# In the gated MLP of an encoder block, GpSimd makes the third convolution tap, most sums of values and two of three weight sums

## The chip, the cores and the metric

One core of one Trainium2 chip runs the whole kernel. The metric is the device time of an execution in microseconds (us), the median over runs. The engines are TensorE (PE; its weight loads are PEld), VectorE (DVE), ScalarE (ACT), GpSimd (POOL) and SyncE (SP), which issues nearly all DMAs.

## What is computed

An encoder block on 272 tokens (256 and 16 meta tokens) of width 2048, all in float32: a normalised input projection, neighbourhood attention on 8 heads and latent attention on 8 heads, an output projection, and a gated MLP of width 5632 with a convolution over positions on the gate. The change lies in the MLP:

```python
def conv_glu(x, w_gate, w_up, conv_w, conv_b, w_down):
    g = x @ w_gate
    u = x @ w_up
    gp = jnp.pad(g, ((0, 0), (pad, pad), (0, 0)))
    gc = conv_b
    for i in range(CONV_W):                 # CONV_W = 3 taps
        gc = gc + conv_w[i] * gp[:, i:i + L]
    return (jax.nn.silu(gc) * u) @ w_down
```

## The kernel before

**Numbers in two parts.** Every float32 product is made of matmuls on a high part (`hi`, `whi`: ScalarE rounds to the matmul's type) and a low part (`lo`, `wlo`: VectorE subtracts the high part from the value). A product takes three matmuls (`mm3`, L734 to L736; `product3` through `MM`, L291) or two (`mm2`, L2056 and L2057). So each weight that is loaded (tiles `raw`) is read once by ScalarE (`split_hi`, the helper at L251) and once by VectorE (`split_lo`, the helper at L255) before TensorE may use it. There are 4 buffers each for `whi` and `wlo` and 5 for `raw`; a buffer is given back when TensorE has used the piece.

**Products with sums.** Twenty of the 44 tiles of the up projection are made in five groups of four ("quads", `QUADS`), and most of the down projection in a similar way, by a scheme that multiplies 2 x 2 blocks with seven products instead of eight. For that it needs sums of weights and sums of the other operand. `weight_sums` (L633 on) makes, for each of 8 row pairs of a quad, one sum on 512 columns and two on 256 columns in a tile of the slots `made` (before the change one tile, `more_raw`); this tile is then split like a loaded weight. `value_sums` makes the sums of the MLP's values for the down projection: four operations on 128 columns and, after ScalarE's high parts, two subtractions on 256 columns into the tile `sums`, which a DMA saves (`pair_sums` calls it for each pair of value tiles; the sums of the last pairs, from `LAST - 3` on, are needed soon after). The sums of the normalised input are made once, by `hl_sums`; some are kept in room of the tile `act` that is not yet in use (`near`), others are saved and loaded again when a row pair needs them. `near_to(g)` says for how many quads pair `g` finds its sums in `near`.

**The MLP's work.** The list `work` interleaves, for each quad, the 16 pieces of its row pairs with the gate and up pieces of other tiles; `lead, tail = 3, 2` pieces of the latter stand ahead and behind. For a gate tile, `gated` scales the matmuls' result from PSUM into an `mt` tile (12 slots); `convolved` then makes the three taps (ScalarE, and two `scalar_tensor_tensor` on VectorE at L263) and the Silu. `tile_up` or, for a quad, `seven` (which combines the seven products), four transposes on TensorE each (`TR`, L297) and `quad_value` make the value, and `finish_value` splits it into `act`.

**What sets the order.** Each engine runs its instructions in the order in which they are written. That order comes from `Flow`, a planner in Python: it runs all these pieces of work as threads, gives every operation a cost in ns and writes next whichever can start first. `PTT` (GpSimd) costs 90 ns and 2.7 ns a column, 3.9 ns from 400 us on; VectorE's `TT` costs 68 ns and 1.04 ns a column whatever GpSimd does. A step of TensorE that depends on another engine is planned 700 ns behind it (`TO_PE`). A matmul's cost before the change is 0.445 ns a column and 3 ns.

## Time and profile before

| | us |
|---|---|
| median of three runs | 1103.25 |
| the runs | 1102.38, 1103.25, 1103.39 |
| span of the profiled execution (first to last instruction) | 1102.0 |
| TensorE busy | 1094.0 |
| VectorE busy | 1015.0 |
| ScalarE busy | 751.1 |
| GpSimd busy | 120.8 |

The profile was taken in an execution of its own, whose only time is its span. The attention and the output projection fill the first 395 us, the quads with their gate and up tiles lie between about 400 and 820 us, and the down projection ends the kernel. Rows of a group have the line, engine and operation, the tiles, the shapes and the count, then busy time in us, the mean of one in ns, and after the second bar the engine's idle time ahead of them. Rows of a stretch have its bounds and length, then busy time and count of PE, PEld, DVE, ACT and POOL, the granted clock, and the DMA engines' share and rate. In an order, the number behind an underscore tells tiles of one kind apart, "x2" means twice in a row, and the first field is the line in that kernel (helpers: L255 before is L260 after, L263 is L268, L279 is L284, L291 is L299, L734 to L736 are L743 to L745).

### The profile page before, as it was taken

What the parts mean: (1) busy time and instruction counts of PE and PEld (TensorE: products, weight loads), DVE (VectorE), ACT (ScalarE), POOL (GpSimd) and SP (SyncE); (2) the same over time, 40 slices, a digit from 0 to 9 for tenths busy, and PEclk for the clock granted to TensorE, in tenths of its full rate; (3) what the DMA queues carried; (4) which work ended last, traced back from release to release, by engine and by line L of the source; (5) the groups of instructions that cost most, each with busy time, mean ns of one, the idle gap of its engine ahead of it and who ended that gap; (6) DMA issues with size and microseconds to landing.
All of it is one profiled execution on the core that took longest, in us unless ns stands there. A gap on an engine that the chain in (4) does not pass through costs nothing.

```text
span 1102.0 us, 22408 instructions
## 1 busy us (share of the span) xinstructions
PE 1094.0 (99%) x8164; PEld 1046.5 (95%) x8164; DVE 1015.0 (92%) x1935; ACT 751.1 (68%) x1507; POOL 120.8 (11%) x199
## 2 busy tenths in 40 slices
PE   9999999999999999999999999999999999999998
PEld 9999999999999999999999999999999999888887
DVE  8969887988878989999999999999999989999997
ACT  8688978888646776656666666665666656566663
POOL 3211222232443400000000000000000000000001
PEclk9999999999999999999999999999999999999999
DMA  9765678567877778655666656758788878699891
GB/s 327 253 230 176 197 218 236 149 203 182 255 207 208 229 256 324 215 193 192 224 221 209 225 192 237 262 193 285 264 299 287 292 237 322 205 320 336 302 331 45
DMA packets 82166, 262.72 MB, mean 238 GB/s; under 512 B 9224, under 2 KB 13320, under 8 KB 82056
## 3 DMA queue, kind: packets, MB, share of 16 engines
q1 hardware_dynamic: 78600, 252.38, 66.0%
q0 software_dynamic: 3168, 8.65, 5.2%
q8 instruction: 64, 1.05, 0.4%
q14 instruction: 46, 0.38, 0.1%
q10 hardware_dynamic: 288, 0.27, 0.1%
HBM read 243.82 MB, written 34.08 MB: 252 GB/s over the span
## 4 chain that ended last, share of the span: by engine, by line
PE 87%; ACT 5%; DVE 4%; DMA 2%; issue 1%; SPq 0%; POOL 0%; DVEq 0%; ACTq 0%; POOLq 0%
PE bank L291 27%; PE bank L734 14%; PE bank L735 14%; PE bank L736 14%; PE bank L2056 11%; PE bank L2057 6%; PE bank L297 2%; ACT whi L251 1%; DVE wlo L255 1%; DVE scr L263 1%; ACT scr L251 1%; DMA scr<-scr 1%; ACT qraw L251 0%; DMA early<-in_w_down_s 0%; DMA raw<-in_w_cq 0%
## 5 line engine op out<-in xcount | busy, mean ns | idle before, releaser
L251 ACT ACTIVATE whi<-raw 128x512 fp32r<-128x512 f32 (+2 forms) x493 | 354.1, 738 | 158.5 <-PE bank L735 54.6
L255 DVE TENSOR_TENSOR wlo<-raw,whi 128x512 fp32r<-128x512 f32 (+2 forms) x493 | 408.0, 848 | 30.7 <-ACT whi L251 29.8
L734 PE MATMUL bank<-hl,whi 128*128 128x258 f32 (+1 forms) x1208 | 347.8, 288 | 0.1
L735 PE MATMUL bank<-hl,whi 128*128 128x258 f32 (+1 forms) x1208 | 343.7, 285 | 0.0
L736 PE MATMUL bank<-hl,wlo 128*128 128x258 f32 (+1 forms) x1208 | 343.1, 284 | 0.2 <-DVE wlo L255 0.2
L736 PEld LDWEIGHTS bank<-hl,wlo 128*128 128x128 f32 x1208 | 229.7, 190 | 0.6 <-DVE wlo L255 0.4
L735 PEld LDWEIGHTS bank<-hl,whi 128*128 128x128 f32 x1208 | 229.3, 190 | 0.1
L734 PEld LDWEIGHTS bank<-hl,whi 128*128 128x128 f32 x1208 | 228.2, 189 | 0.8 <-ACT scr L251 0.3
L291 PE MATMUL bank<-whi,act 128*128 128x256 f32 (+1 forms) x574 | 143.5, 302 | 0.0
L2056 PE MATMUL bank<-hl,whi 128*128 128x512 f32 x384 | 136.6, 395 | 0.0
L2057 PE MATMUL bank<-hl,wlo 128*128 128x256 f32 x384 | 107.7, 280 | 0.0
L291 PEld LDWEIGHTS bank<-whi,act 128*128 128x128 f32 x574 | 100.2, 189 | 5.2
L251 ACT ACTIVATE whi<-more_raw 128x1024 fp32r<-128x1024 f32 x69 | 71.8, 1040 | 42.7 <-DVE more_raw L255 22.7
L291 PE MATMUL bank<-wlo,act 128*128 128x256 f32 (+1 forms) x287 | 86.8, 302 | 0.0
L2056 PEld LDWEIGHTS bank<-hl,whi 128*128 128x128 f32 x384 | 72.1, 188 | 14.9
L255 DVE TENSOR_TENSOR wlo<-more_raw,whi 128x1024 fp32r<-128x1024 f32 x69 | 82.6, 1196 | 3.2 <-ACT whi L251 3.1
L279 POOL TENSOR_TENSOR halves<-halves,resT 128x256 f32<-128x256 f32 x4 | 3.0, 784 | 703.9 <-ACT halves L251 703.9
L2057 PEld LDWEIGHTS bank<-hl,wlo 128*128 128x128 f32 x384 | 72.4, 188 | 0.0
L291 PE MATMUL bank<-whi,sin 128*128 128x256 f32 (+1 forms) x248 | 69.0, 325 | 0.0
L251 ACT ACTIVATE whi<-halves 128x1024 fp32r<-128x1024 f32 (+2 forms) x57 | 52.2, 936 | 22.4 <-PE bank L291 7.5
L255 DVE TENSOR_TENSOR wlo<-halves,whi 128x1024 fp32r<-128x1024 f32 (+2 forms) x57 | 60.4, 1074 | 0.5 <-ACT whi L251 0.3
L291 PEld LDWEIGHTS bank<-wlo,act 128*128 128x128 f32 x287 | 54.3, 189 | 2.2
(323 smaller groups left out, 2216.1 us busy)
## 6 DMA issues: line engine op xcount, KB each, us to landing
raw<-in_w_gate SPq DMA_DIRECT2D x88, 512.0 KB, 5.1
raw<-in_w_in SPq DMA_DIRECT2D x52, 512.0 KB, 4.5
raw<-in_w_up SPq DMA_DIRECT2D x48, 512.0 KB, 4.5
raw<-in_w_up_s SPq DMA_DIRECT2D x40, 512.0 KB, 4.4
raw<-in_w_out SPq DMA_DIRECT2D x32, 512.0 KB, 5.1
sin<-s_down SPq DMA_DIRECT2D x28, 512.0 KB, 6.5
raw<-in_w_down_m SPq DMA_DIRECT2D x21, 512.0 KB, 5.4
s_down<-sums SPq DMA_DIRECT2D x20, 512.0 KB, 6.5
```

The costliest lines, as they stand in the source:

```text
L251: nc.scalar.activation(out, in_, f, **kw)
L255: nc.vector.tensor_tensor(out, a, b, op)
L263: nc.vector.scalar_tensor_tensor(out, a, s, b, op0, op1)
L279: nc.gpsimd.tensor_tensor(out, a, b, op)
L291: nc.tensor.matmul(o, l, r, start=start, stop=stop)
L297: nc.tensor.transpose(o, i, ident[:n, :n])
L734: nc.tensor.matmul(ps, whi, xhi, start=start, stop=False)
L735: nc.tensor.matmul(ps, whi, xlo, start=False, stop=False)
L736: nc.tensor.matmul(ps, wlo, xhi, start=False, stop=stop)
L2056: nc.tensor.matmul(ps, whi, x, start=start, stop=False)
L2057: nc.tensor.matmul(ps[:, :n], wlo, x[:, 0, :], start=False, stop=stop)
```

## The change

Four edits go together. GpSimd makes the third tap's addition (after a new scaled copy on ScalarE), the value sums of all pairs below `LAST - 3`, and the two weight sums on 256 columns of each up pair. `made` gets a second tile, `more_sums`, in the room where the kept sums of pair 2 lay (`SUMS_IN`); those are saved and loaded in every quad instead, and the activation tiles 32 and 33 get a tile of their own (`act_two`) there once the last quad's sums are used (`sums_out`). The lead and tail of a quad are 2 and 1 pieces. The planner's cost of a matmul on 256 columns or more is `stream(n)`.

```diff
+SUMS_IN = 2
...
 def near_to(g):
+    if g == SUMS_IN:
+        return 0
     return sum(f <= FC - KC + 2 * g for f in (*QUADS, MID)[1:])
...
+    def stream(n):
+        return n / 2.4 + 0.436 * -(-n // 16) + 4.7
...
-        return 0.445 * n + 3 if n >= 256 else max(0.84 * n, 0.84 * m, 27)
+        return stream(n) if n >= 256 else max(0.84 * n, 0.84 * m, 27)
...
-        lead, tail = 3, 2
+        lead, tail = 2, 1
...
             yield from TT(t[:, : 2 * q], raw[:, q : 3 * q], raw[:, : 2 * q], ALU.add)
             fl.set(r.summed[0])
-            yield from TT(t[:, 2 * q : 3 * q], raw[:, 2 * q : 3 * q], t[:, :q], ALU.add)
-            yield from TT(t[:, 3 * q :], t[:, 2 * q : 3 * q], raw[:, 3 * q :], ALU.add)
+            op = PTT if r.of == "up" else TT
+            yield from op(t[:, 2 * q : 3 * q], raw[:, 2 * q : 3 * q], t[:, :q], ALU.add)
+            yield from op(t[:, 3 * q :], t[:, 2 * q : 3 * q], raw[:, 3 * q :], ALU.add)
...
-        act = mpool.tile([P, FC, 2, SEQ], F32R, name="act")
+        tile_of = mpool.tile([P, FC - 2, 2, SEQ], F32R, name="act")
+        f = FC - KC + 2 * SUMS_IN
+        act = [tile_of[:, i - 2 * (i > f)] for i in range(FC)]
...
+        near[SUMS_IN] = mpool.tile([P, PW], F32, tag="act_two", name="more_sums")
+        fl.put(made, near[SUMS_IN])
...
-        yield from STT(
-            gc[:, 1:SEQ], gs[:, : SEQ - 1], vec("conv2", f), gc[:, 1:SEQ], ALU.mult, ALU.add
-        )
+        yield from ACT(gs[:, : SEQ - 1], gs[:, : SEQ - 1], AF.Copy, scale=vec("conv2", f))
+        yield from PTT(gc[:, 1:SEQ], gc[:, 1:SEQ], gs[:, : SEQ - 1], ALU.add)
         yield from ACT(gs[:, :SEQ], g_, AF.Silu)
...
     def pair_sums(g):
         pair = [values[i] for i in (2 * g, 2 * g + 1)]
-        yield from value_sums(*saved_sums["down"][g], *(t[:, :SEQ] for t in pair))
+        op = PTT if g < LAST - 3 else TT
+        yield from value_sums(*saved_sums["down"][g], *(t[:, :SEQ] for t in pair), TT=op)
...
+    def sums_out():
+        for t in (yield made, 2):
+            if t is not near[SUMS_IN]:
+                fl.put(made, t)
+        f = FC - KC + 2 * SUMS_IN
+        t = mpool.tile([P, 2, 2, SEQ], F32R, tag="act_two", name="act_two")
+        act[f : f + 2] = [t[:, i] for i in range(2)]
+        fl.set(ev_far[SUMS_IN])
```

`value_sums` and `split_plain` take the helper as an argument `TT` and use it for all six operations. `mm2` and `mm3` are costed by `stream` as well.

The end of a quad on VectorE, before: three splits (`wlo`), the combinations of the seven products from PSUM (`bank`) into `raw_82` and `mt`, and then the three weight sums of a pair of the next quad.

```order
L255 TENSOR_TENSOR raw_82<-bank_74,mt_5445 128x256
L255 TENSOR_TENSOR mt_5445<-bank_73,mt_5445 128x256
L255 TENSOR_TENSOR wlo_89<-raw_80,whi_85 128x1024
L255 TENSOR_TENSOR mt_5445<-bank_73,mt_5445 128x256
L255 TENSOR_TENSOR raw_82<-bank_77,mt_5445 128x256
L255 TENSOR_TENSOR raw_82<-bank_74,raw_82 128x256
L255 TENSOR_TENSOR wlo_90<-raw_83,whi_86 128x1024
L255 TENSOR_TENSOR raw_82<-bank_77,mt_5445 128x256
L255 TENSOR_TENSOR raw_82<-mt_5445,bank_75 128x256
L255 TENSOR_TENSOR more_raw_5449<-raw_81 128x512
L255 TENSOR_TENSOR more_raw_5449<-raw_81,more_raw_5449 128x256
L255 TENSOR_TENSOR more_raw_5449<-more_raw_5449,raw_81 128x256
```

The same place of a quad on VectorE now:

```order
L260 TENSOR_TENSOR more_raw_5472<-raw_84 128x512
L260 TENSOR_TENSOR wlo_89<-raw_80,whi_85 128x1024
L260 TENSOR_TENSOR wlo_90<-raw_81,whi_86 128x1024
L260 TENSOR_TENSOR raw_82<-bank_77,mt_5468 128x256
L260 TENSOR_TENSOR mt_5468<-bank_76,mt_5468 128x256
L260 TENSOR_TENSOR mt_5467<-bank_76,mt_5468 128x256
L260 TENSOR_TENSOR wlo_91<-raw_84,whi_87 128x512
L260 TENSOR_TENSOR raw_82<-bank_79,mt_5468 128x256
L260 TENSOR_TENSOR wlo_91<-raw_84,whi_87 128x256
L260 TENSOR_TENSOR raw_82<-bank_77,raw_82 128x256
L260 TENSOR_TENSOR raw_82<-bank_79,mt_5467 128x256
L260 TENSOR_TENSOR raw_82<-mt_5467,bank_72 128x256
```

The two sums on 256 columns are gone, the first sum of the next quad's first pair stands ahead of the combinations, and two splits of 1024 columns and one of 768 stand ahead of or between them. TensorE's transposes read `raw_82` right after the last row; they stood 40 matmuls behind the quad's last product (20 of 512 and 20 of 256 columns), and now stand 44 behind it (16 and 16 of these, and 12 of 258): 15,360 columns before, 15,384 now.

GpSimd had nothing between its last addition of the attention part (`kr`, 387 us) and the last four of the kernel (`halves`). Now it has, at the end of a quad, third taps (255 columns), weight sums (`more_raw`, `more_sums`) and value sums (128 columns, then `sums`) in this order:

```order
L284 TENSOR_TENSOR more_sums<-raw_81,more_sums 128x256
L284 TENSOR_TENSOR more_sums<-more_sums,raw_81 128x256
L284 TENSOR_TENSOR mt_5469<-mt_5469,mt_5468 128x255 x2
L284 TENSOR_TENSOR more_raw_5472<-raw_84,more_raw_5472 128x256
L284 TENSOR_TENSOR more_raw_5472<-more_raw_5472,raw_84 128x256
L284 TENSOR_TENSOR more_sums<-raw_80,more_sums 128x256
L284 TENSOR_TENSOR more_sums<-more_sums,raw_80 128x256
L284 TENSOR_TENSOR mt_5468<-mt_5467,mt_5468 128x128
L284 TENSOR_TENSOR mt_5467<-mt_5467 128x128
```

A quad has 28 such operations on 255 or 256 columns and 12 on 128. In all GpSimd gets 232 and VectorE loses 232.

The new matmul costs also move TensorE's rows in the attention part. Around the sum of squares of the first keys (`nak` with `ones_r`), before:

```order
L734 MATMUL bank_72<-hl_100,whi_86 128x272
L735 MATMUL bank_72<-hl_100,whi_86 128x272
L736 MATMUL bank_72<-hl_100,wlo_90 128x272
L291 MATMUL bank_76<-nak_260,ones_r 128x272 x2
L734 MATMUL bank_74<-hl_100,whi_86 128x272
L735 MATMUL bank_74<-hl_100,whi_86 128x272
```

And now:

```order
L743 MATMUL bank_74<-hl_99,whi_85 128x272
L744 MATMUL bank_74<-hl_99,whi_85 128x272
L745 MATMUL bank_74<-hl_99,wlo_89 128x272
L299 MATMUL bank_76<-nak_260,ones_r 128x272 x2
L743 MATMUL bank_72<-hl_99,whi_85 128x272
L744 MATMUL bank_72<-hl_99,whi_85 128x272
```

The sum now stands 15 rows of the program earlier, among the products of another input tile. TensorE has the same number of matmuls of each size in both orders.

More of the change, by code (lines that the diff above doesn't have):

```diff
@@ L732, in mm3 @@
         whi, wlo = yield from block()
-        yield "pe", 3 * (0.445 * size(xhi) + 3)
+        yield "pe", 3 * stream(size(xhi))
         nc.tensor.matmul(ps, whi, xhi, start=start, stop=False)
@@ L1155, in encoder_block, with split_plain @@
     ev_sum_a, ev_sum_b = Event(), Event()
-    def split_plain(hi, lo, src):
+    def split_plain(hi, lo, src, TT=TT):
         yield from ACT(hi, src, AF.Copy)
@@ L1914, in mlp_buffers @@
             f = FC - KC + 2 * i
-            near[i] = act[:, f : f + 2].rearrange("p f i t -> p (f i t)").bitcast(F32)
+            t = tile_of[:, f - 2 * (i > SUMS_IN) :][:, :2]
+            near[i] = t.rearrange("p f i t -> p (f i t)").bitcast(F32)
+        near[SUMS_IN] = mpool.tile([P, PW], F32, tag="act_two", name="more_sums")
+        fl.put(made, near[SUMS_IN])
         fl.set(ev_mlp)
         for i, (dst, saved) in enumerate(saved_sums["up"][:EARLY]):
+            if i == SUMS_IN:
+                continue
             yield saved
@@ L1962, in finish_value @@
             yield ev_far[(f - FC + KC) // 2]
-        yield from ACT(act[:, f, 0, :], u_, AF.Copy)
-        yield from TT(act[:, f, 1, :], u_, act[:, f, 0, :].bitcast(F32), ALU.subtract)
+        yield from ACT(act[f][:, 0, :], u_, AF.Copy)
+        yield from TT(act[f][:, 1, :], u_, act[f][:, 0, :].bitcast(F32), ALU.subtract)
         fl.set(ev_act[f])
@@ L1976, in encoder_block, with value_sums @@
     values, last_S = {}, {g: ([], Event()) for g in (LAST - 1, LAST)}
-    def value_sums(dst, saved, a, b, place=None):
+    def value_sums(dst, saved, a, b, place=None, TT=TT):
         (A11, A21), (A12, A22) = ((t[:, :P], t[:, P:SEQ]) for t in (a, b))
@@ L1990, in value_sums @@
         for i, t in enumerate((a, b)):
-            yield from split_plain(hl_[:, i], hl_[:, 2 + i], t)
+            yield from split_plain(hl_[:, i], hl_[:, 2 + i], t, TT)
         if last:
@@ L2054, in mm2 @@
         whi, wlo = yield from block()
-        yield "pe", 347
+        yield "pe", stream(2 * SEQ) + stream(SEQ)
         nc.tensor.matmul(ps, whi, x, start=start, stop=False)
@@ L2086, in mlp_weights @@
                     if which < KC - ST - 1:
-                        yield from mm2(ps, act[:, f], SEQ, f == 0, f == FC - 1)
+                        yield from mm2(ps, act[f], SEQ, f == 0, f == FC - 1)
                     else:
                         yield from mm3(
-                            ps[:, :SEQ], act[:, f, 0, :], act[:, f, 1, :], f == 0, f == FC - 1
+                            ps[:, :SEQ], act[f][:, 0, :], act[f][:, 1, :], f == 0, f == FC - 1
                         )
@@ L2134, in scheme_products @@
                 k += 2 * r.g
-                A = hl[k] if r.of == "up" else act[:, k]
+                A = hl[k] if r.of == "up" else act[k]
                 a = [A[:, j, h * P : (h + 1) * P] for j in range(2)]
@@ L2178, in scheme_products @@
                     fl.spawn(quad_out(r.quad, r.order, P7, dict(sum_banks)))
+                    if r.quad == QUADS[-1]:
+                        fl.spawn(sums_out())
+    def sums_out():
[6 more added lines that the diff above has]
+        fl.set(ev_far[SUMS_IN])
     def seven(order, P7, b, U):
```

## Prediction

> **What bounds the kernel now.** I read the page first, then the busy time in three stretches, then TensorE's own waits.
>
> ```profile
> span 1102.0 us, 22408 instructions
> PE 1094.0 (99%) x8164; PEld 1046.5 (95%) x8164; DVE 1015.0 (92%) x1935; ACT 751.1 (68%) x1507; POOL 120.8 (11%) x199
> ...
> 0.00:300.00 300.00, 295.94 (x2405) 291.45 (x2406) 257.74 (x652) 247.67 (x732) 82.61 (x161) 1.00 0.72 220
> 300.00:1050.00 750.00, 750.00 (x5489) 713.24 (x5488) 711.91 (x1227) 475.96 (x742) 35.15 (x35) 1.00 0.73 250
> 1050.00:1102.00 52.00, 48.03 (x274) 41.84 (x272) 45.38 (x58) 27.51 (x35) 3.05 (x4) 0.99 0.50 178
> ...
> PE bank L291 <- POOL sq8r L279: 1.1, 3, 0.7
> PE bank L866 <- DVE em L863: 1.1, 1, 1.1
> PE bank L291 <- DVE late L255: 0.9, 1, 0.9
> ```
>
> The columns of a stretch are its length and then PE, PEld, DVE, ACT and POOL busy time with counts. TensorE is busy for every one of the 750 us from 300 to 1050, at the full granted clock. It is idle 4.06 us in the first 300 and 3.97 us in the last 52, where the span ends in evictions and output. Its waits on others all lie in the attention part. So VectorE, however busy, does not set the time: removing work from it can give nothing back in the MLP, where TensorE never waits. Anything that makes TensorE wait there is added to the time in full.
>
> VectorE is nevertheless nearly full. The MLP repeats every 66.7 us, one quad of up tiles each time:
>
> ```profile
> 482.50:549.20 66.70, 66.70 (x530) 65.29 (x529) 65.66 (x122) 42.77 (x68) 0.00 (x0) 1.00 0.58 200
> 549.20:615.90 66.70, 66.70 (x530) 65.25 (x529) 65.66 (x122) 42.81 (x67) 0.00 (x0) 1.00 0.62 215
> 615.90:682.60 66.70, 66.70 (x530) 65.29 (x529) 65.66 (x122) 42.76 (x67) 0.00 (x0) 1.00 0.61 213
> ...
> POOL halves L279 <- ACT halves L251: 703.9, 2, 702.6
> L251 ACT ACTIVATE whi<-raw 128x1024 fp32r<-128x1024 f32 x16 | 17.0, 1061 | 13.3 <-PE bank L291 6.2 <-PE bank L2056 2.8 <-PE bank L735 2.6
> ```
>
> VectorE works 65.66 of 66.7 us per quad, TensorE 66.7. GpSimd sits idle for the 703.9 us of the MLP. In a quad ScalarE's splits wait mostly for TensorE to free a split buffer, which says that the split weights run ahead of TensorE and not behind.
>
> **What leaves VectorE.** The groups of one quad, with count, busy time and mean ns:
>
> ```profile
> L255 DVE TENSOR_TENSOR wlo<-raw,whi 128x512 fp32r<-128x512 f32 x8 | 5.5, 684 | 0.0
> L255 DVE TENSOR_TENSOR more_raw<-more_raw,raw 128x256 f32<-128x256 f32 x8 | 3.4, 424 | 0.2
> L255 DVE TENSOR_TENSOR more_raw<-raw,more_raw 128x256 f32<-128x256 f32 x8 | 3.4, 424 | 0.3
> L255 DVE TENSOR_TENSOR mt<-mt 128x128 f32<-128x128 f32 x12 | 3.4, 288 | 0.1
> L255 DVE TENSOR_TENSOR mt<-bank,mt 128x256 f32<-128x256 f32 x8 | 3.0, 418 | 0.1
> L255 DVE TENSOR_TENSOR sums<-mt,sums 128x256 fp32r<-128x256 f32 x6 | 2.5, 419 | 0.0
> L263 DVE SCALAR_TENSOR_TENSOR mt<-mt,vecs,mt 128x255 f32<-128x255 f32 x4 | 1.9, 484 | 0.1
> L263 DVE SCALAR_TENSOR_TENSOR mt<-mt,vecs 128x255 f32<-128x255 f32 x2 | 1.0, 484 | 0.1
> L251 ACT ACTIVATE mt<-mt,vecs 128x256 f32<-128x256 f32 x6 | 3.3, 594 | 1.3 <-DVE mt L255 1.3
> ```
>
> Per quad the change takes away two of three weight sums (3.4 + 3.4), the twelve subtractions and additions of values on 128 columns (3.4), their six low parts (2.5) and six third taps (1.9 + 1.0): 15.6 us. All 20 groups of this quad add to 74.5 us against 65.66 us of union, because consecutive instructions overlap at their ends, so what comes free is 15.6 x 65.66 / 74.5 = 13.8 us. ScalarE gains six scaled copies, at most 594 ns each, 3.6 us on 42.8 of 66.7: nothing waits for that. GpSimd gets 28 operations on 255 or 256 columns and 12 on 128 columns per quad, 232 in all.
>
> **What GpSimd's work does to VectorE.** No GpSimd addition runs in the quads of this trace. The nearest rows are the output projection, where GpSimd adds the residual while VectorE splits weights. VectorE from 300 to 345, GpSimd in the same stretch, and VectorE from 345 to 400:
>
> ```profile
> L255 DVE TENSOR_TENSOR wlo<-raw,whi 128x512 fp32r<-128x512 f32 x31 | 25.1, 844 | 1.7 <-ACT whi L251 1.7
> L263 DVE SCALAR_TENSOR_TENSOR scr<-scr,scr 128x258 f32<-128x258 f32 x1 | 0.9, 862 | 0.0
> L255 DVE TENSOR_TENSOR parts_sq<-sum_a,parts_sq 128x258 fp32r<-128x258 f32 x1 | 0.9, 851 | 0.0
> ...
> L279 POOL TENSOR_TENSOR res<-res,scr 128x258 f32<-128x258 f32 x13 | 11.9, 934 | 20.7 <-DVE scr L255 20.7
> L279 POOL TENSOR_TENSOR kr<-kr,scr 128x258 f32<-128x258 f32 x1 | 2.0, 1980 | 6.1 <-ACT scr L251 6.1
> ...
> L255 DVE TENSOR_TENSOR wlo<-raw,whi 128x512 fp32r<-128x512 f32 x18 | 13.0, 742 | 0.0
> L255 DVE TENSOR_TENSOR raw<-raw 128x128 f32<-128x128 f32 x16 | 9.0, 563 | 0.3
> L263 DVE SCALAR_TENSOR_TENSOR hl<-res,vecs,hl 128x258 fp32r<-128x258 f32 x14 | 7.8, 586 | 0.0
> L255 DVE TENSOR_TENSOR scr<-bank,sum_a 128x258 f32<-128x258 f32 x12 | 4.5, 416 | 0.0
> ```
>
> The same 128x512 split that takes 684 ns in a quad takes 844 here, and a 128x128 operation 563 instead of 288: VectorE is held up while GpSimd reads. Operations that read PSUM and one SBUF tile are not (416 here, 418 in a quad). From 300 to 345: 31 x 160 ns + 2 x 0.44 us = 5.8 us over 14 additions, 0.42 us each. From 345 to 400: 18 x 58 + 16 x 275 + 14 x 106 ns = 6.9 us over the other 14 of the 15 kr additions, 0.49 us each. I take 0.45 us per addition of 256 columns (between the two) and half, 0.22 us, for one of 128 columns (no row; 0.1 to 0.45). Ends for the 256: 0, if GpSimd always falls on VectorE's idle or PSUM-reading time, and 0.49.
>
> Sum per quad: 65.66 - 13.8 + 28 x 0.45 + 12 x 0.22 = 67.1 us if nothing is covered, against 66.7. VectorE would have 14.8 us of idle time and about 19 PSUM reads of some 0.42 us for GpSimd to fall on, so part is covered; a quarter makes it 63.3. So on average VectorE's load comes back almost to what it was: **the gain is eaten by the hold-ups**, and neither engine becomes a clear bound. GpSimd itself takes 28 x 0.93 to 1.24 plus 12 x at most 0.93, 31 to 46 us of 66.7.
>
> The Trainium skill, "SBUF — State Buffer", section "Who interferes with whom", says that a VectorE instruction with two SBUF inputs and a GpSimd instruction that reads SBUF contend for a shared port, and that the later one blocks fully until the first is done. The trace agrees on which instructions contend and shows 0.42 to 0.49 us blocked, not the 0.93 us that GpSimd's addition lasts.
>
> **Where TensorE could wait.** The planner prices GpSimd's operations on GpSimd alone; it does not know that they stretch VectorE's. Whatever place in the written order has little spare time is then missed. The tightest that I find is the end of a quad: TensorE transposes the quad's result, in its fixed order, right after VectorE has combined the seven products.
>
> ```profile
> 556.90 0.41 DVE L255 TENSOR_TENSOR raw<-mt,bank 128x256 f32<-128x256 f32 x1
> ...
> 558.13 0.60 PE L297 MATMUL bank<-ident,raw 128*128 128x128 f32 x4
> ```
>
> The last combination ends at 557.31, the transposes start at 558.13: 0.82 us to spare. By the new order the transposes stand at the same distance behind the last product (15,384 columns of matmuls instead of 15,360); in between VectorE has the combinations (which read PSUM and are not held up) and four splits, 3.2 us, that are. GpSimd has two weight sums and two third taps queued at that place. Three of the four falling on those splits makes 3 x 0.45 = 1.35 us of delay, 0.53 us more than there is to spare. None gives 0; four, and a last weight sum late behind the value sums, at most 1.6. Five quads: **5 x 0.53 = 2.7 us** (0 to 8), with all TensorE matmuls behind them pushed back.
>
> **Edits at nothing.** The second place for sums lets two pairs of weight sums be in work, so the longer chain (two GpSimd additions of 0.93 to 1.24 us for two of 0.42) starts a pair earlier; a pair is 8 us of TensorE, which covers the extra 1 to 1.7 us. The price is that the kept sums of one pair are loaded in all five quads, not in one: four more 512 KB loads on SP's queue, landing in about 5 us at a DMA share of 0.58 to 0.62, issued with the pair's weights; if not covered, up to 1 us each. The third tap lengthens the gate's chain by one ScalarE and one GpSimd operation, some 1.5 us, and its user stands a pair later. The two activation tiles that wait for the second place are needed after the last quad. The shorter lead before a quad moves TensorE's work without adding any: the matmul count is equal.
>
> The refit of matmul costs reorders the attention part too. Its 4.06 us of idle time hold the 1.1 us behind the first memset, which stays; the rest may move either way by about 2 us. I take 0.
>
> Sum: span 1102.0 + 2.7 = 1104.7. The median of the runs, 1103.25, is 1.25 above this execution's span, which makes 1106.0 us. A measurement of this kernel can tell about 0.2%, 2.2 us, from no change.
>
> **Rivals.**
>
> *No change.* GpSimd's additions fall on VectorE's new idle time and the 0.82 us at each quad's end absorbs the rest. For it: VectorE gets 13.8 us per quad back, the split buffers run ahead, TensorE had no wait at all with VectorE at 98%. Against: the order is fixed, and nothing was planned for the hold-up. Time 1103.3.
>
> *Faster, by the attention part.* The new matmul costs set another order in the first 300 us. If the new order drops the waits on `sq8r` and `late` (2.0 us) and part of the 1 us beside them, and the quads stay without waits: 1103.25 - 2.7 = 1100.5. It decides for faster once these waits are gone and the quads' ends wait under 0.1 us each. Against: small operations placed by another order usually find other waits.
>
> *VectorE becomes the bound.* If additions cost 0.49 us, those of 128 columns 0.45 and nothing is covered: 65.66 - 13.8 + 13.7 + 5.4 = 71.0 us, 4.3 over 66.7 in each of five quads, some of it made up in the buffers: about 15 us, 1118. It decides from 0.43 us per addition uncovered, but needs cover to fail, while VectorE's freed time offers it.
>
> *Whole blocking.* By the page's rule as a mechanism here, each addition would hold VectorE for its full 0.93 us and half of that for 128 columns: 65.66 - 13.8 + 26 + 5.6 = 83.5 us per quad, 16.8 over, 1187. The rows of 0.42 and 0.49 speak against it.
>
> **How the numbers follow.** Waits at the quads' ends of 0.45 to 1.4 us each: 0.35, own range 1105.5 to 1110. No change: 0.32. Faster: 0.20. VectorE as the bound: 0.11. Whole blocking: 0.02. So slower 0.48, within 0.2% 0.32, faster 0.20. The range from 1100.0 to 1116.0 leaves out half of the third rival, the last one, and the better part of the attention's luck beyond 3 us.
>
> **What would show it.** In the changed profile: VectorE busy 62 to 66 us per 66.7 again, with its 128x512 splits at 750 to 850 ns instead of 684; GpSimd 31 to 46 us; waits of TensorE's transposes on VectorE's `raw`, about half a microsecond, five times; the stretch from 300 to the last quad longer by 2 to 4 us. It would be wrong if TensorE stays without waits in the quads (no change), if waits on split weights or weight sums recur through the quad (VectorE or GpSimd as the bound), or if the difference comes before 300 us.

## The result and the profile after

The changed kernel takes 1120.84 us, 1.56% longer than the kernel before: ratio 1.0156, 95% interval 1.0142 to 1.0169, about 17.5 us. The forecast was 1106.0, and its range ended at 1116.0. The sign was right, the size was not. One execution of a later run (all sums of weights back on VectorE) took 1777.43 us at a granted clock of 0.556, and that run's median leaves it out.

The profiled execution of the changed kernel, first its page, then stretches in the same columns as before: the attention part, the quads (400 to 850 us holds them in both kernels), one quad, and that quad in two pieces, the first of them the 28 us behind the transposes that end the quad before (they start at 499.23).

```profile
span 1118.1 us, 22476 instructions
PE 1101.5 (99%) x8164; PEld 1048.2 (94%) x8164; DVE 1009.8 (90%) x1703; ACT 762.7 (68%) x1551; POOL 377.6 (34%) x431
...
0.00:300.00 300.00, 293.79 (x2365) 286.98 (x2366) 257.11 (x647) 244.95 (x727) 79.68 (x158) 1.00 0.71 217
400.00:850.00 450.00, 443.34 (x3414) 428.00 (x3413) 415.61 (x555) 290.26 (x486) 252.43 (x226) 1.00 0.71 236
499.00:568.50 69.50, 67.73 (x530) 65.48 (x529) 63.83 (x81) 43.64 (x74) 46.18 (x40) 1.00 0.65 212
499.00:527.00 28.00, 26.67 (x223) 26.46 (x222) 27.62 (x36) 18.70 (x36) 23.27 (x25) 1.00 0.61 202
527.00:568.50 41.50, 41.06 (x309) 39.02 (x308) 36.21 (x46) 24.94 (x40) 22.91 (x16) 1.00 0.68 218
```

The kernel before, one stretch that was not shown:

```profile
400.00:850.00 450.00, 450.00 (x3500) 437.52 (x3499) 436.33 (x805) 288.16 (x458) 0.00 (x0) 1.00 0.68 238
```

Read the counts behind PE, not only its busy time. TensorE has 8164 matmuls in both kernels, so a matmul that is missing in a stretch is lost time. In the first 300 us there are 2365 for 2405: 40 x 300 / 2405 = 5.0 us. From 400 to 850 there are 3414 for 3500: 86 x 450 / 3500 = 11.1 us. Together 16.1 us, which is all of the difference of the spans, 1118.1 - 1102.0. (Busy time shows only 2.2 and 6.7 us, since the rows of matmuls overlap and a short wait hides in that.) So there are **two losses in two places**: the attention part, and the quads. 530 matmuls, a quad, took 66.7 us and now take 69.5. VectorE does not look full there, 63.83 us of 69.5, but in the 28 us behind the transposes it is busy 27.62.

Ahead of 300 us the largest wait of TensorE in the changed kernel is one that the kernel before does not have, for GpSimd's `p`:

```profile
PE bank L305 <- POOL p L284: 1.9, 4, 0.8
```

It is part of the 5.0 us; where the rest of them lies stays open. TensorE's waits of the changed kernel from 400 to 850 us:

```profile
PE bank L745 <- DVE wlo L260: 5.7, 7, 1.3
PE bank L299 <- DVE wlo L260: 0.7, 3, 0.2
PE bank L2073 <- DVE wlo L260: 0.2, 1, 0.2
```

All of them are for low parts of weights, none for the `raw` of a quad's end. The rows of the changed kernel around the first large wait, and around the second transposes behind it, those of the five with the least to spare:

```profile
520.54 1.48 DVE L260 TENSOR_TENSOR wlo<-more_raw,whi 128x1024 fp32r<-128x1024 f32 x1
522.02 1.93 DVE L260 TENSOR_TENSOR wlo<-raw,whi 128x512 fp32r<-128x512 f32 x2
523.87 1.23 DVE L260 TENSOR_TENSOR more_raw<-raw 128x512 f32<-128x512 f32 x1
525.03 1.21 DVE L260 TENSOR_TENSOR wlo<-raw,whi 128x1024 fp32r<-128x1024 f32 x1
...
519.68 3.98 POOL L284 TENSOR_TENSOR mt<-mt,mt 128x128 f32<-128x128 f32 x4
...
524.67 0.29 PE L744 MATMUL bank<-hl,whi 128*128 128x258 f32 x1
526.29 0.39 PE L745 MATMUL bank<-hl,wlo 128*128 128x258 f32 x1 [1.33 <-DVE wlo L260]
...
637.34 0.41 DVE L260 TENSOR_TENSOR raw<-mt,bank 128x256 f32<-128x256 f32 x1
638.03 1.04 PE L305 MATMUL bank<-ident,raw 128*128 128x128 f32 x8
```

The split ends at 525.03 + 1.21 = 526.24, and TensorE reads it at 526.29, 1.62 us behind the start of its last matmul; a matmul's pitch is 66.7 / 530 = 0.13 us. Ahead of it VectorE works without a gap, and next to GpSimd's additions its operations are long: a 512-column sum takes 1.23 us, where before it took 0.69. At the transposes, where the prediction put the wait, 0.28 us are still to spare (637.75 to 638.03).

The same groups of VectorE after, and GpSimd's, from 430 to 790 us:

```profile
L260 DVE TENSOR_TENSOR wlo<-raw,whi 128x1024 fp32r<-128x1024 f32 x84 | 117.2, 1402 | 8.1 <-ACT whi L256 7.8
L260 DVE TENSOR_TENSOR wlo<-raw,whi 128x512 fp32r<-128x512 f32 x41 | 39.3, 959 | 7.8 <-ACT whi L256 7.7
L260 DVE TENSOR_TENSOR mt<-bank,mt 128x256 f32<-128x256 f32 x42 | 16.2, 416 | 1.1 <-ACT mt L256 0.8
...
L284 POOL TENSOR_TENSOR mt<-mt,mt 128x255 f32<-128x255 f32 x29 | 42.2, 1474 | 31.5 <-ACT mt L256 31.5
L284 POOL TENSOR_TENSOR sums<-mt,sums 128x256 fp32r<-128x256 f32 x29 | 30.7, 1063 | 2.9 <-ACT sums L256 2.9
```

A 128x512 split takes 959 ns for 684, more than the 844 of the output projection. An operation with one operand in PSUM keeps its 416. And the two that meet slow each other: GpSimd's additions take 1063 to 1474 ns here, the quickest of 256 columns in the same stretch 729 (`more_sums`).

### The profile page after: what moved, and what is told of

Same layout as the page of the kernel before. It is cut to its first block, busy times and chain, and to the rows that moved or that the text cites. A ratio compares the mean times of both kernels' runs of the same rounds, so it can differ in the third digit from the quotient of the medians.

```text
span 1118.1 us, 22476 instructions
## 1 busy us (share of the span) xinstructions
PE 1101.5 (99%) x8164; PEld 1048.2 (94%) x8164; DVE 1009.8 (90%) x1703; ACT 762.7 (68%) x1551; POOL 377.6 (34%) x431
## 4 chain that ended last, share of the span: by engine, by line
PE 69%; DVE 11%; POOL 8%; ACT 6%; issue 3%; DMA 3%; SPq 0%; DVEq 0%; ACTq 0%; POOLq 0%
PE bank L299 21%; PE bank L745 11%; PE bank L743 11%; PE bank L744 11%; PE bank L2072 10%; PE bank L2073 5%; DVE wlo L260 5%; POOL mt L284 5%; ACT whi L256 3%; PE bank L305 2%; DMA scr<-scr 1%; POOL more_raw L284 1%; DVE scr L268 1%; ACT scr L256 1%; DVE mt L260 1%
## 5 line engine op out<-in xcount | busy, mean ns | idle before, releaser
L260 DVE TENSOR_TENSOR wlo<-raw,whi 128x512 fp32r<-128x512 f32 (+2 forms) x494 | 449.1, 933 | 48.5 <-ACT whi L256 47.0
L299 PE MATMUL bank<-whi,act 128*128 128x256 f32 (+1 forms) x532 | 133.7, 303 | 0.0
L284 POOL TENSOR_TENSOR mt<-mt,mt 128x255 f32<-128x255 f32 (+1 forms) x72 | 77.2, 1082 | 101.2 <-ACT mt L256 71.7
L299 PEld LDWEIGHTS bank<-whi,act 128*128 128x128 f32 x532 | 92.9, 189 | 5.2
L299 PE MATMUL bank<-wlo,act 128*128 128x256 f32 (+1 forms) x266 | 81.0, 305 | 0.7 <-DVE wlo L260 0.7
L299 PE MATMUL bank<-whi,sin 128*128 128x256 f32 (+1 forms) x280 | 76.1, 320 | 0.0
L256 ACT ACTIVATE whi<-more_raw 128x1024 fp32r<-128x1024 f32 (+1 forms) x49 | 50.4, 1029 | 28.7 <-PE bank L2073 12.8
L260 DVE TENSOR_TENSOR wlo<-more_raw,whi 128x1024 fp32r<-128x1024 f32 (+1 forms) x49 | 66.5, 1358 | 3.8 <-ACT whi L256 3.7
L256 ACT ACTIVATE mt<-mt,vecs 128x256 f32<-128x256 f32 (+1 forms) x88 | 44.9, 547 | 36.4 <-DVE mt L260 19.6
L284 POOL TENSOR_TENSOR mt<-mt 128x128 f32<-128x128 f32 (+1 forms) x44 | 34.9, 794 | 85.3 <-ACT mt L256 80.0
```

Of the source, the lines that this page charges most:

```text
L256: nc.scalar.activation(out, in_, f, **kw)
L260: nc.vector.tensor_tensor(out, a, b, op)
L284: nc.gpsimd.tensor_tensor(out, a, b, op)
L299: nc.tensor.matmul(o, l, r, start=start, stop=stop)
```

## The experiments

Three theories. **A**: VectorE is held up while GpSimd reads, and the splits come late. **B**: what is late is GpSimd's own chain, sums and taps that others wait for in order, not VectorE's operations. **C**: the planner's new matmul costs lose time on their own. For each run the ratio to the kernel before on the same chip with its 95% interval; "matmuls missing" is counted as above, against the profile before.

### The four edits taken apart

The new costs alone, put into the kernel before (`mm3` and `mm2` likewise):

```diff
+    def stream(n):
+        return n / 2.4 + 0.436 * -(-n // 16) + 4.7
...
-        return 0.445 * n + 3 if n >= 256 else max(0.84 * n, 0.84 * m, 27)
+        return stream(n) if n >= 256 else max(0.84 * n, 0.84 * m, 27)
```

> The kernel before, with only the planner's new costs of a matmul (the function stream and its three uses); no work changes its engine. Three theories stand. Theory A: GpSimd's reads hold VectorE's adds up, and where GpSimd's sums and taps bunch behind a quad's end the splits of the weights come late: about 11 us in quads 2 to 5. Theory B: what is late is GpSimd's own chain (a sum made slowly and in order, the split behind it waiting), not VectorE's held-up adds: the same 11 us. Theory C, beside either: the new costs reorder the part up to 300 us, about 4.7 us. C expects about 1108 us here, with all of the loss ahead of 300 us and a quad still at 66.7 us. If C is false the time stays at 1103 us. A and B expect nothing of this run in the quads.

Measured: 1114.07 us, ratio 1.0100 (1.0085 to 1.0115), 10.9 us. Stretches and waits of this run, the waits from 400 us on:

```profile
0.00:300.00 300.00, 293.81 (x2366) 287.10 (x2367) 257.33 (x647) 245.13 (x728) 80.26 (x158) 1.00 0.71 217
400.00:850.00 450.00, 447.13 (x3469) 433.69 (x3468) 430.48 (x794) 283.33 (x456) 0.00 (x0) 1.00 0.70 236
```

```profile
PE bank L739 <- DVE wlo L255: 2.9, 6, 1.2
```

39 matmuls are missing ahead of 300 us (4.9 us), as in the changed kernel, but 31 in the quads as well (4.0 us), with GpSimd idle there. C holds and is larger than it was stated: 1108 us had been expected.

The converse, the changed kernel with the old costs (the same lines the other way):

> The kernel after, with the planner's old costs of a matmul. Theory C (the new costs lose 4.7 us ahead of 300 us) expects about 1116 us, TensorE's idle time of 0 to 300 us back at about 4.1 us, and the quads still at about 69.5 us, as theories A and B have it. If the new costs also made the bunch behind a quad's end, the quads return to 66.7 us and the time to 1103 to 1105 us.

Measured: 1109.34 us, ratio 1.0058 (1.0043 to 1.0073), 6.2 us.

```profile
0.00:300.00 300.00, 296.60 (x2406) 291.89 (x2407) 257.67 (x652) 247.51 (x733) 82.18 (x161) 1.00 0.73 220
400.00:850.00 450.00, 445.47 (x3453) 431.78 (x3452) 420.08 (x569) 293.31 (x491) 254.96 (x228) 1.00 0.71 238
```

Nothing is missing ahead of 300 us, 47 matmuls (6.0 us) in the quads. Both forecasts of the time are missed: the quads lose less than with the new costs, but not nothing. The two parts, 10.9 and 6.2, add to 17.1 of the 17.5 us. So the move of work itself costs a third, and the costs in the planner, which look like bookkeeping, two thirds.

Then one part of the move at a time back to VectorE, with the new costs kept. All sums of values:

```diff
-        op = PTT if g < LAST - 3 else TT
+        op = TT
```

> The kernel after, with all sums of values made by VectorE again; GpSimd keeps the third tap and the two weight sums. Theory A: GpSimd has 18 adds fewer in a quad (6 of 256 columns, 12 of 128), so some 5 us of hold-ups go and some 5 us of VectorE's own work come back at a priority that lets the splits go first: the bunch is thinner, and 5 to 11 of the 11 us in the quads go, 1110 to 1115 us. Theory B, if the sums of values in GpSimd's queue are what makes its taps and weight sums late: 1109 to 1111 us; if it is the weight sums by themselves: 1120 us still.

Measured: 1116.52 us, 1.0120 (1.0105 to 1.0135); 43 and 55 matmuls missing (5.4 and 7.1 us). All sums of weights:

```diff
-            op = PTT if r.of == "up" else TT
+            op = TT
```

> The kernel after, with all sums of the up weights made by VectorE again; GpSimd keeps the third tap and the sums of values. Theory A: 16 of the 28 adds of 256 columns in a quad go from GpSimd, some 7 us of hold-ups, against some 6 us of VectorE's own work that comes back: most of the loss in the quads goes, 1109 to 1113 us. Theory B: the split behind a weight sum waits for VectorE alone, so all of the 11 us go if the weight sums were what was late (1109 us), and none go if the taps or the sums of values were (1120 us).

Measured: 1117.60 us, 1.0127 (1.0107 to 1.0148); 56 and 61 missing (7.0 and 7.8 us). Of the 86 matmuls missing in the quads, 31 are missing with the new costs alone; of the other 55 the first run recovers 31 and the second 25, about half each. Both expectations were missed, since they did not count on the loss that the new costs make in the quads. They do not tell A from B.

### Held up, or late?

The kernel before, with 40 additions on GpSimd that nobody needs, one behind each first sum of up weights:

```diff
+            if r.of == "up" and idle:
+                fl.spawn(idle[0](t))
...
+        def idle_op(t):
+            yield "pool", 1090
+            nc.gpsimd.tensor_tensor(spare, spare, t[:, :SEQ], ALU.add)
```

> The kernel before, VectorE keeping all of its work; beside it GpSimd makes 40 adds of 128x256 that nobody needs (8 in a quad), each behind a row's first sum of up weights, and no other engine's order changes. Theory A (the hold-up itself): each add takes about 0.45 us from a VectorE that is busy 49.2 us of 50 from 500 to 750 us, so 8 x 0.45 = 3.6 us in a quad that has 1.1 us to spare, less what lies in VectorE's gaps: a quad of 68.5 to 69.2 us for 66.7, and 1111 to 1116 us in all. Theory B (only waiting for GpSimd's results counts): nobody waits for these, 1103 us.

Measured: 1116.91 us, ratio 1.0126 (1.0111 to 1.0141): 14.0 us for 40 additions that nobody waits for. Its quads and TensorE's waits there, then one of the additions with VectorE beside it, and the group of the second VectorE row from 430 to 790 us:

```profile
400.00:850.00 450.00, 438.47 (x3398) 424.72 (x3397) 438.84 (x780) 274.33 (x441) 39.82 (x40) 1.00 0.68 229
```

```profile
PE bank L740 <- DVE wlo L255: 11.4, 9, 1.6
```

```profile
500.53 0.42 DVE L255 TENSOR_TENSOR more_raw<-raw,more_raw 128x256 f32<-128x256 f32 x1
500.99 0.84 DVE L255 TENSOR_TENSOR more_raw<-more_raw,raw 128x256 f32<-128x256 f32 x1
...
500.57 0.98 POOL L1918 TENSOR_TENSOR spare<-spare,more_raw 128x256 f32<-128x256 f32 x1 [8.50 <-DVE more_raw L255]
...
L255 DVE TENSOR_TENSOR more_raw<-more_raw,raw 128x256 f32<-128x256 f32 x41 | 31.2, 760 | 1.2
```

Two equal VectorE additions stand one behind the other. The first starts 0.04 us ahead of GpSimd's and keeps its 0.42 us; the second starts while GpSimd's runs and takes 0.84. That is the hold-up, by itself: 0.42 us by an addition of 0.98 us. 102 matmuls are missing in the quads, 13.1 us or 0.33 us for each addition, so most of it goes through to the end. B expected nothing here; the time lies just above A's range.

The same with fills in the place of the additions:

```diff
-            nc.gpsimd.tensor_tensor(spare, spare, t[:, :SEQ], ALU.add)
+            nc.gpsimd.tensor_tensor(spare[:, :4], spare[:, :4], t[:, :4], ALU.add)
+            for _ in range(3):
+                nc.gpsimd.memset(spare[:, 4:], 0.0)
```

> As the run with the adds that nobody needs, but in the place of each add GpSimd adds 4 columns and then fills the tile three times with zeros, so that it is busy about as long and reads hardly anything. Theory A, with the reads as the cause: VectorE's 128x1024 splits keep their 1.22 us and the time stays at 1103 us. If GpSimd's writes hold VectorE as its reads do: 1111 to 1116 us again.

Measured: 1102.64 us, ratio 0.9997 (0.9987 to 1.0006), no matmul missing in the quads. The same group of VectorE and the fills:

```profile
L255 DVE TENSOR_TENSOR more_raw<-more_raw,raw 128x256 f32<-128x256 f32 x44 | 18.7, 425 | 1.3
...
L1920 POOL MEMSET spare<- 128x252 f32 x119 | 36.7, 308 | 4.6
```

The second addition takes 425 ns, as in the kernel before, where it took 760 beside GpSimd's additions: GpSimd busy and writing costs VectorE nothing; GpSimd reading does. The Trainium skill, "SBUF — State Buffer", section "Who interferes with whom", says of a VectorE instruction with two SBUF inputs that it contends with a GpSimd instruction that reads and not with one that only writes: these two runs agree, with 760 ns beside the reads and 425 beside the fills.

Last, the changed kernel with the old costs, its order and waits kept, but its reads taken away (it leaves out the taps and sums that GpSimd makes):

```diff
+        mlp = fl.cur.t >= 4e5 and out.shape[0] == P and size(out) in (P, SEQ, SEQ - 1)
...
-        nc.gpsimd.tensor_tensor(out, a, b, op)
+        if not mlp:
+            nc.gpsimd.tensor_tensor(out, a, b, op)
+            return
+        nc.gpsimd.tensor_tensor(out[:, :4], a[:, :4], b[:, :4], op)
+        for _ in range(2 if size(out) == P else 3):
+            nc.gpsimd.memset(out[:, 4:].bitcast(F32), 0.0)
```

> The kernel after with the planner's old costs of a matmul (1109.3 us), in which each of GpSimd's adds in the MLP is replaced by an add of 4 columns and two or three fills with zeros (taps, sums of values and sums of weights are not computed); order, dependences and roughly the durations stay, the reads go. Theory A: the hold-ups go and with them nearly all of the 6.2 us, 1103 to 1105 us. Theory B: GpSimd's results come as late as before, 1108 to 1110 us.

Measured: 1103.64 us, ratio 1.0007 (0.9998 to 1.0017).

```profile
500.00:566.70 66.70, 66.70 (x530) 65.29 (x530) 52.87 (x82) 43.74 (x74) 45.50 (x150) 1.00 0.67 222
400.00:850.00 450.00, 449.76 (x3496) 437.18 (x3495) 365.78 (x576) 297.44 (x497) 263.36 (x826) 1.00 0.71 242
```

4 matmuls missing for 47, and GpSimd as busy (263 us for 255): without GpSimd's reads the move loses nothing. **A holds.** B alone falls, but GpSimd's chain does carry part of the delay. One of the four large waits of the run with the old costs, engine by engine:

```profile
503.87 1.27 POOL L284 TENSOR_TENSOR mt<-mt 128x128 f32<-128x128 f32 x1 [0.76 <-DVE act L260]
519.15 0.42 ACT L256 ACTIVATE mt<-mt 128x256 f32<-128x256 f32 x1 [1.53 <-POOL mt L284]
519.48 1.04 ACT L256 ACTIVATE whi<-raw 128x1024 fp32r<-128x1024 f32 x1
519.32 1.13 DVE L260 TENSOR_TENSOR more_raw<-raw 128x512 f32<-128x512 f32 x1
520.55 1.31 DVE L260 TENSOR_TENSOR wlo<-raw,whi 128x1024 fp32r<-128x1024 f32 x1
521.91 0.39 PE L745 MATMUL bank<-hl,wlo 128*128 128x258 f32 x1 [0.78 <-DVE wlo L260]
```

The same place in the run without reads:

```profile
501.05 0.20 POOL L288 TENSOR_TENSOR mt<-mt 128x4 f32<-128x4 f32 x1 [0.36 <-ACT whi L256]
516.22 0.42 ACT L256 ACTIVATE mt<-mt 128x256 f32<-128x256 f32 x1 [3.54 <-POOL mt L290]
517.62 1.23 DVE L260 TENSOR_TENSOR wlo<-raw,whi 128x1024 fp32r<-128x1024 f32 x1 [3.57 <-ACT whi L256]
519.00 0.29 PE L751 MATMUL bank<-hl,wlo 128*128 128x258 f32 x1
```

Two paths end at the late split within 0.07 us of each other: VectorE is free at 520.45, and ScalarE's high part, which stands behind a tap of GpSimd, is done at 520.52. GpSimd works on end up to that tap, 15.25 us with the reads and 15.14 without, so it is not its own pace that differs. It starts later, behind VectorE's `act`: 8.43 us behind the quad's transposes (495.44) for 7.58 (493.47). The other three waits of this kind are like it (GpSimd starts at 8.7 us for 7.6). The fills last as long as the held-up additions, so what GpSimd's own slowing costs is not shown. So VectorE's hold-ups delay the split twice, directly and by way of GpSimd and ScalarE; in the changed kernel VectorE came last (free at 525.10, the high part done at 524.03). Even without reads this order leaves the split 0.15 us (518.85 to 519.00).

The run without reads shows two things more. VectorE works 365.78 us for 436.33 before, and the kernel is not faster: that is all that this move could have brought with no hold-up. And with the reads, in the run of the old costs, VectorE works 420.08 us at nearly the same instructions (569 for 576): of the 70.6 us that left VectorE, the hold-ups gave 54.3 back.

### Is it the place, and can the planner mend it?

The planner was told of the hold-up (old costs otherwise):

```diff
         nc.gpsimd.tensor_tensor(out, a, b, op)
+        if fl.cur.t > 4e5:
+            fl.clock["dve"] += 1.7 * size(out)
```

> The kernel after with the planner's old costs of a matmul, and a planner that charges VectorE with 435 ns for each of GpSimd's 256-column adds in the MLP (half of that for 128 columns). Theory A in its local form (on average VectorE has the time, only the planner's order doesn't know of the hold-ups where they bunch): the order leaves room for them, and most of the 6.2 us go, 1103 to 1106 us. If VectorE with its hold-ups is the bound of the whole quad, an order can't help: 1108 to 1110 us.

Measured: 1111.98 us, ratio 1.0084 (1.0067 to 1.0101), 60 matmuls missing in the quads (7.7 us). It did not help; the order that it led to has its waits in other places, 2.2 us of them one wait of a piece of the up projection for VectorE's `mt`.

GpSimd's sums only outside of the 30 us behind a quad's end, and only inside, taps in both (the condition is the other way round in the second; `fl.quad_end` is the planner's time of a quad's last product):

```diff
+    def in_time():
+        return not 0 <= fl.cur.t - fl.quad_end < 30e3
...
-            op = PTT if r.of == "up" else TT
+            op = PTT if r.of == "up" and in_time() else TT
...
-        op = PTT if g < LAST - 3 else TT
+        op = PTT if g < LAST - 3 and in_time() else TT
```

> The kernel after with the planner's old costs of a matmul, where VectorE makes the sums of weights and of values that fall, by the planner's clock, into the 30 us behind a quad's end, and GpSimd only those outside of it, with all taps. Local theory (the hold-ups cost where VectorE works without a gap behind a quad's end and the lead of its splits falls from 7 us to nothing): nearly all of the 6.2 us go, 1103 to 1105 us. If the hold-ups cost wherever they fall: some 40 per cent of the sums are left, 1105 to 1107 us.

> The converse: GpSimd makes the sums of weights and of values that fall into the 30 us behind a quad's end and all taps, VectorE those outside. Local theory: the loss of the whole move stays, 1108 to 1111 us, with TensorE's waits 20 to 30 us behind a quad's end. If the hold-ups cost wherever they fall: about 60 per cent of 6.2 us, 1106 to 1107.5 us.

Measured: 1107.58 us, 1.0043 (1.0026 to 1.0059) outside; 1108.38 us, 1.0053 (1.0038 to 1.0068) inside. One of four similar waits of each, the sums outside first:

```profile
542.69 0.39 PE L750 MATMUL bank<-hl,wlo 128*128 128x258 f32 x1 [0.56 <-DVE wlo L260]
```

```profile
519.44 0.39 PE L750 MATMUL bank<-hl,wlo 128*128 128x258 f32 x1 [0.63 <-DVE wlo L260]
```

The wait moves with the additions: some 48 us behind a quad's transposes with the sums outside the stretch, some 26 us behind them with the sums inside. The second run came as the local theory had it, the first did not, so the theory that only the stretch behind a quad's end is tender falls. Each half also costs nearly as much as the whole (5.0 and 5.8 us against 6.2); VectorE gets its own work back where GpSimd's is taken away, which may be why.

How much of it can be moved at all: with the old costs, all sums of values on VectorE (the first of these edits), and then all sums on VectorE and the tap alone on GpSimd (both).

```diff
-        op = PTT if g < LAST - 3 else TT
+        op = TT
...
-            op = PTT if r.of == "up" else TT
+            op = TT
```

> The kernel after with the planner's old costs of a matmul and all sums of values on VectorE (22 adds of 256 columns a quad stay on GpSimd). Theory A, the hold-ups where VectorE's lead is thin, without the new costs: of the 6.2 us that 40 adds a quad cost, about half is left, 1105 to 1107 us, and TensorE's waits in the quads are still for splits of weights. If the loss goes only with the last add: 1108 us and more; if VectorE was relieved enough: 1103 us.

> The kernel after with the planner's old costs of a matmul, and GpSimd making the third tap alone (6 adds of 255 columns a quad). Theory A: 6 x 0.45 = 2.7 us of hold-ups in place of 2.8 us of VectorE's own work, spread over a quad: 1103 to 1104.5 us. No theory expects less than 1102 us, since TensorE is busy all the time from 300 to 1050 us before.

Measured: 1109.67 us, 1.0060 (1.0043 to 1.0077) with 22 additions a quad, and 1103.43 us, 1.0004 (0.9994 to 1.0013) with the six taps. 22 additions cost as much as 40, six cost nothing: the loss does not follow the count, and the expectation of about half was missed. In the run with 22, 2.1 of TensorE's 3.9 us of waits in the quads are one wait in the first quad, longer than any in the run with 40.

### The planner's costs

The kernel before with one part of the new costs each, the weight blocks first (`mm3`, `mm2`), then all others (`cost`):

```diff
-        yield "pe", 3 * (0.445 * size(xhi) + 3)
+        yield "pe", 3 * stream(size(xhi))
...
-        yield "pe", 347
+        yield "pe", stream(2 * SEQ) + stream(SEQ)
```

```diff
-        return 0.445 * n + 3 if n >= 256 else max(0.84 * n, 0.84 * m, 27)
+        return stream(n) if n >= 256 else max(0.84 * n, 0.84 * m, 27)
```

> The kernel before with the new planner costs for the weight blocks alone (the two places that charge a whole block), all other matmuls at the old costs. A block of gate or up goes from 353 to 359 ns in the plan, one of down from 347 to 350 ns. If the blocks' costs make the loss: 1111 to 1115 us, with 0.4 us waits in each quad; if not: 1103 us.

> The converse: the new planner costs for all matmuls but the weight blocks (attention, and the products of the quads' sums). If these make the loss ahead of 300 us: 1106 to 1109 us with quads of 66.7 us; if the blocks alone did it: 1103 us.

Measured: 1109.91 us, 1.0068 (1.0053 to 1.0083) for the weight blocks; 1106.52 us, 1.0032 (1.0020 to 1.0044) for all others. Stretches of the first, then of the second:

```profile
0.00:300.00 300.00, 294.46 (x2379) 288.00 (x2380) 255.38 (x648) 246.60 (x728) 79.99 (x158) 1.00 0.72 218
400.00:850.00 450.00, 447.35 (x3468) 433.87 (x3467) 430.65 (x795) 283.45 (x455) 0.00 (x0) 1.00 0.71 236
```

```profile
0.00:300.00 300.00, 294.95 (x2395) 290.48 (x2396) 258.57 (x651) 247.84 (x731) 80.98 (x160) 1.00 0.72 219
400.00:850.00 450.00, 450.00 (x3501) 437.57 (x3500) 435.57 (x803) 287.07 (x457) 0.00 (x0) 1.00 0.71 238
```

The blocks' costs make all of the loss in the quads (32 matmuls, 4.1 us) and 26 matmuls, 3.2 us, of that ahead of 300 us; the others make none in the quads and 10 matmuls, 1.2 us, ahead of 300 us. 7.3 and 3.9 us add to 11.2, near the 10.9 of both. Of the 3.9 us 2.7 are not located: the profiled execution spans 1103.3 us, 1.3 more than before. The blocks' loss in the quads lies ahead of 500 us (733 matmuls for 767 from 400 to 500); the waits of some 0.3 us in each later quad, which had been expected of them, are in the run with both costs only.

Two runs asked why, both of the kernel before: one with the new costs and a longer step to TensorE, one with the old costs made 1.5% lower (`mm3` and `mm2` likewise).

```diff
-    TO_PE, FROM_PE, OTHER = 700.0, 200.0, 140.0
+    TO_PE, FROM_PE, OTHER = 1200.0, 200.0, 140.0
```

```diff
-        return 0.445 * n + 3 if n >= 256 else max(0.84 * n, 0.84 * m, 27)
+        return 0.438 * n + 3 if n >= 256 else max(0.84 * n, 0.84 * m, 27)
```

> The kernel before with the planner's new costs of a matmul, and the planner's step from another engine to TensorE at 1200 ns for 700. Theory C2: in the quads the new costs (each matmul 1 to 2 ns dearer) take the last 0.4 us off the lead of one split a quad; 500 ns more of planned lead would bring it back, the quads lose nothing and the time goes from 1114.1 to 1108 to 1110 us (what is ahead of 300 us stays or changes by 2 us). If the split is late because VectorE's order ahead of it changed, a longer step doesn't help: 1112 to 1116 us.

> The kernel before with the planner's matmul costs 1.5 per cent lower (0.438 ns a column for 0.445, 342 ns for 347). Theory C2: the new costs lose because they are higher, so that the planner sees time for the splits that TensorE doesn't leave; lower costs then keep or raise the lead in the quads, 1101 to 1104 us. If any change of the costs upsets an order that was found by trial, the time rises here too, 1106 us and more.

Measured: 1109.51 us, 1.0056 (1.0041 to 1.0071); in the quads 18 matmuls are missing (2.3 us), and four waits of up to 0.4 us for a split are still there. And 1106.09 us, 1.0025 (1.0016 to 1.0035), with no matmul missing in either stretch; its profiled execution spans 1103.0 us, 1.0 more than before, and has a new wait of 0.9 us for a split in the down projection. Lower costs keep the quads whole and yet end 2.7 us later. A longer step mends part: the time is in the range that was expected of it, but the quads were to lose nothing. Which of VectorE's rows the dearer blocks put ahead of the late split, no run shows; it stays open.

No run was faster than the kernel before beyond its interval.

## Why the prediction was wrong, point by point

Two steps failed. The larger is the term for the planner's costs, taken at 0: they make 10.9 of the 17.5 us. The other is the place where TensorE would wait, the transposes, with 2.7 us: it waits for splits of weights, and the move loses 6.2 us.

- **TensorE bounds the kernel, so work taken from VectorE brings nothing.** Right: in the run without reads VectorE has 70 us less to do from 400 to 850 us and the time is the same within 0.2%.
- **13.8 us leave VectorE per quad.** About right: 52.87 us are left of 65.66 in the run without reads, 12.8 fewer.
- **0.45 us of hold-up for an addition of 256 columns.** Right where one meets a busy VectorE: 0.42 measured by itself. Over all 228 operations of GpSimd from 400 to 850 us, those of 128 columns among them, the run with the old costs gave back 54.3 us, 0.24 each; the sum has 0.38 each if nothing is covered, so more than its quarter was.
- **"The refit of matmul costs reorders the attention part too... I take 0".** This step failed, and it is the larger error: 5.0 us there, where about 2 either way had been allowed. That the same costs would also make TensorE wait in the quads (4.0 us) was not considered at all.
- **"The tightest that I find is the end of a quad", 0.82 us, 5 x 0.53 = 2.7 us.** This step failed too: wrong place and too small. The transposes never wait in the changed kernel. What was tighter was in the trace before: a split for a gate tile, with 0.46 us to spare, in rows of the kernel before:

```profile
541.52 1.22 DVE L255 TENSOR_TENSOR wlo<-raw,whi 128x1024 fp32r<-128x1024 f32 x1
...
543.20 0.28 PE L736 MATMUL bank<-hl,wlo 128*128 128x258 f32 x1
```

  It ends at 542.74, and TensorE reads it at 543.20, 51.7 us behind the transposes. The new costs alone make TensorE wait here (at 550.70 in their run, 52.2 us behind them). The move itself waits at another split for a gate tile, 26 to 27 us behind them, to which the changed order leaves 0.15 us even without hold-ups; the trace before could not show that one. The reading that "the split weights run ahead of TensorE" came from the group of ScalarE's splits, which wait for a buffer most of the time; it says nothing of the narrowest.
- **The sum over a quad, "neither engine becomes a clear bound".** Its number held, 63.8 us of VectorE in the quad shown, but it says nothing of a wait: an average over 66.7 us was set against a fixed order that leaves a split less than half a microsecond. In the same quad VectorE is busy 27.6 of the first 28 us and idle 5.3 of the other 41.5.
- **The edits at nothing** (second place for sums, four more loads, lead and tail): right with the old costs; the runs without reads and with taps alone contain all of them and lose nothing that can be measured.
- **Rivals.** VectorE as the bound, 1118, came nearest in the number, but by luck: it takes VectorE full over a quad, and VectorE was full for 28 us of it. The range left half of it out, and held no case in which both parts lose. "Faster, by the attention part" looked at the right stretch, which got slower instead. Whole blocking fell (0.42 us of 0.98). The sign was forecast by the mechanism that makes the smaller part of the loss, so it is in part luck.

## What to carry to other kernels

Where a bound engine has no wait at all, look for the narrowest lead of each thing that it reads, not for the load of the engine that makes it; then ask what stretches the rows ahead of that place. Additions moved from a busy VectorE to GpSimd take most of their time back by holding up what stays, 54 of 70 us here. And change a planner's costs in a run of their own: one or two per cent more in a matmul's cost moved the time by 10.9 us, the work that was moved by 6.2.

## What the runs showed of the hardware

- GpSimd's additions are slow in turn: the quickest of 256 columns takes 0.73 us, and the means are 0.99 us in the run of additions that nobody needs and 1.06 to 1.49 us in the changed kernel, where GpSimd works 46 us of a quad.
- A fill by GpSimd, 308 ns for 252 columns, holds VectorE up by nothing that shows (425 ns for an addition of 256 columns with and without, 760 beside GpSimd's additions).
- VectorE's operations with one operand in PSUM keep 416 ns beside GpSimd (418 in the kernel before), so those are the rows to put beside its reads.
